# Queries and keys of a hybrid decoder layer by seven quadrant products (Strassen) on one Trainium2 core

## The chip, the core and the metric

The kernel runs on one core of a Trainium2 chip. The core has a matrix engine (TensorE, PE in the profile, with its weight loads as PEld), a vector engine (VectorE, DVE), an engine for copies and functions (ScalarE, ACT), GpSimd (POOL), and SyncE (SP), which here only issues transfers. The engines run side by side, each takes its own instructions in order, and they wait for one another by semaphores. PE reads from SBUF (on-chip memory of 128 partitions) and writes to PSUM, which has eight banks of 128 x 512 float32. GpSimd doesn't reach PSUM.

The metric is the device time of one execution in microseconds (us). A change of the time is given as after over before, below 1 for faster.

## The reference

One layer with 2048 tokens of width 1024, in float32. The projection is the part that the change touches; the rest of the layer follows it and is longer.

```python
hn = _rmsnorm(h, ln_mix[i])                  # h * rsqrt(mean(h*h) + eps) * gain
z = hn @ w_in[i]                             # (2048, 1024) @ (1024, 2048)
q = z[..., :512].reshape(B, S, 8, 64) * (64 ** -0.5)
k = z[..., 512:1024].reshape(B, S, 8, 64)
v = z[..., 1024:1536].reshape(B, S, 8, 64)
u = z[..., 1536:]
att = _dilated_attention(q, k, v, slopes)    # three window and dilation patterns
pool = _multiscale_pool(u, pool_w[i], pool_scale[i])
h = h + jnp.concatenate([att, pool], axis=-1) @ w_out[i]
...
```

`_multiscale_pool` takes, for four groups of 128 channels, the trailing mean over 2, 4, 8 or 16 tokens minus the token, multiplies it by a 128 x 128 matrix of the group and scales it per channel. After this come a gated MLP with a causal convolution and a gated addition of a per-layer embedding.

## The kernel before

All products are of float32 accuracy, made from three matmuls of a rounded type (float32r): each operand is kept as a high half (a rounded copy, made by ScalarE) and a low half (the operand minus its high half, made by DVE or GpSimd; `split`, L83). `mm3` (L88) adds high by high, high by low and low by high in one PSUM bank, so each product of 128 x 128 by 128 x 512 costs three matmuls, at L89, L90 and L91.

`phase_project` (L170) makes z. x lies transposed, channels on the partitions: eight k tiles of 128 channels by the tokens of a chunk. There are five chunks: two of 256 tokens, so that the start is short, then three of 512. For each chunk four groups of columns of w_in follow one another: 0 for queries, 1 for keys, 2 for values, 3 for the pooled channels (the last chunk takes 3 ahead of 2). A group is a loop over eight k tiles with four PSUM banks open (L303 to L316); in the groups 0, 1 and 3 w_in is the stationary operand and the tokens run past it, in group 2 it is the other way round, so that values come out with tokens on the partitions. A full group has 96 matmuls of 512 columns; in a chunk of 256 tokens the groups 0, 1 and 3 have 96 of 256 columns and group 2 has 48 of 512.

The high and low halves of the weights of groups 0 to 2 are made in the first chunk and stay in SBUF, in the pool a_w (L176), the phase's first; those of group 3 are fetched and split anew for each chunk. `ahead` (L271) keeps the splits three steps ahead of the matmuls and the fetches further. The order of PE, ACT, DVE and POOL in this phase is the order of the program text (L1947); transfers are issued by SP, those of the pooled branch by POOL.

The norm: `square` (L231) adds the squares of the next chunk, one k tile per step of group 1; `scale` (L235) sums them over the partitions with matmuls into the bank st, takes the root on GpSimd and prepares diagonal tiles; `spread_` (L239) spreads the root over the partitions by two matmuls (bc); `norm_a` (L242) multiplies x by it and `norm_b` (L246) makes the halves hnh and hnl, with the norm weight as the scale, one k tile per step of group 3. The first chunk is multiplied without its root, which is applied to the results (L349). A `Ticker` (L59) runs pieces of work some steps after they were entered; `pool_branch` (L410) puts its windowed sums, its halves, its product with pool_w (bank py, L456) and its stores on later steps with it.

After the phase its pools are closed, and attention's pool b_sb (L494) takes the same space in SBUF. Pools are laid one after another, tiles of a pool in the order in which their tags are first asked for, and a new tile waits until all that used its bytes before is done (reuse_waits). `load_qk` (L502) loads queries and keys of a head: qhh, ks, qll, and two tables of distances, fb and nb; the loads of head 0 come first (L748), those of values next.

Of the kernel before, what the change touches and what calls it, by code (L numbers as in the profile page):

```python
# [10 lines left out]
F32 = mybir.dt.float32  # L11
# [6 lines left out]
P = 128  # L18
# [147 lines left out]
ACFG = dict(nk=3, sc=5, ml=[[1,3,5,11],[1,3,5,7]], pq=[], ph=[1,2,4,8], fi=1, mn=[1,2],ld=4, lu=2, la=3, a0=1, low=[[[1, 0], [1, 1], [1, 1], [0, 0]], [[0, 0]] * 4, [[0, 0]] * 4], man=("PE", "ACT", "DVE", "POOL"))  # L166
EN = dict(PE=mybir.EngineType.PE, ACT=mybir.EngineType.Activation, DVE=mybir.EngineType.DVE, POOL=mybir.EngineType.Pool)


def phase_project(tc, g, xT, w_in, pool_w, rcnt):  # L170
    nc = tc.nc
    tk = g.ticker
    NZ, NV = 6, 3
    chunks = [(0, 256), (256, 256)] + [(t, CH) for t in range(CH, S, CH)]
    with ExitStack() as ctx:
        wres = ctx.enter_context(tc.tile_pool(name="a_w", bufs=1, reuse_waits="tile"))  # L176
        sb = ctx.enter_context(tc.tile_pool(name="a_sb", bufs=1, reuse_waits="tile"))
        psum = ctx.enter_context(tc.tile_pool(name="a_ps", bufs=6, space=PSUM, reuse_waits="tile"))
        psum1 = ctx.enter_context(tc.tile_pool(name="a_ps1", bufs=1, space=PSUM, reuse_waits="tile"))

        def small(name):
            return sb.tile([P, CH], F32, tag="raw", bufs=3, name=name)

        def zt(name):
            return sb.tile([P, CH], F32R, tag="z", bufs=NZ, name=name)
# [7 lines left out]
        g.f32r_tile = lambda pool: pool.tile([P, CH], F32R, tag="z", bufs=NZ, name="dg")  # L193

        def fetch(c, grp, k):
            i = (grp * KD + k) % 3 if c == 0 and grp < 3 else 0
            tag, bufs = (("raw", 3), ("wuh", 3), ("wul", 3))[i]
            raw = sb.tile([P, 512], F32R if i else F32, tag=tag, bufs=bufs, name=f"wr{grp}_{k}")
            raw = fp(raw) if i else raw
            nc.sync.dma_start(raw, w_in[k * P : (k + 1) * P, grp * 512 : (grp + 1) * 512])  # L200
            return raw

        def load_w(pool, raw, grp, k, tag, bufs, low=None):
            hi = pool.tile([P, 512], F32R, tag=tag + "h", bufs=bufs, name=f"wh{grp}_{k}")
            lo = pool.tile([P, 512], F32R, tag=tag + "l", bufs=bufs, name=f"wl{grp}_{k}")
            split(nc, hi, lo, raw, low)
            return hi, lo
# [5 lines left out]
        held = {}  # L213

        def loads(c):
            t0, n = chunks[c]
            st = Shared()
            st.n, st.xs, st.hn = n, [], []
            st.acc = sb.tile([P, CH], F32, tag="acc", name="acc")
            for hf in range(2):  # L220
                xt = sb.tile([P, 4, CH], F32, tag="x", bufs=2, name=f"x{c}_{hf}")
                m = 2 if c == 0 else 4
                for a in range(0, 4, m):
                    ka = slice(4 * hf + a, 4 * hf + a + m)
                    nc.sync.dma_start(xt[:, a : a + m, :n], xT[ka, :, t0 : t0 + n].rearrange("k p t -> p k t"))
                    if c == 0:
                        fetch_to(2 * hf + a // 2)
                st.xs += [xt[:, k, :] for k in range(4)]
            return st

        def square(st, k):  # L231
            eng = nc.gpsimd if st is first and k % 2 else None
            add_square(nc, sb, st.acc, st.xs[k][:, : st.n], k == 0, 1, zt if st is first else None, eng)

        def scale(st):  # L235
            st.pw = rms_scale(nc, g, psum1.tile([P, CH], F32, tag="st", name="st"), st.acc, st.n)
# [1791 lines left out]
```

## Time and profile before

| | |
|---|---|
| time, median of 3 runs | 2394.97 us (2390.77 to 2396.05) |
| the profiled execution | 2395.75 us, of which the span of the trace is 2394.0 |
| mean granted clock of PE | 0.987 |
| the projection phase in the trace | from 6.27 us (first matmul) to 400.07 (first matmul of attention) |
| matmuls with output z | 480 at each of L89 to L91 with tokens moving, 128 each with w_in moving |

The profile is of one execution. "Busy" is the time in which an engine has an instruction in work; PE's matmuls overlap, so that one of 512 columns is listed with some 390 ns though the next starts sooner. A row of a group gives line, engine and operation, output<-inputs by the names of the program, shapes and count, then busy time and mean duration, then idle time just ahead of it and what ended it. A row of the order in time gives start, duration, engine, line and operation, and in brackets the idle time before.

### The profile page before, as it was taken

Reading aid. Unit: us, or ns where it says so; the run is one execution under the profiler, and the core shown is the slowest. Engines: PE = TensorE matmul, PEld = TensorE weight load, DVE = VectorE, ACT = ScalarE, POOL = GpSimd, SP = SyncE. Lnnn points to the kernel's source line nnn. Section 1 sums busy time; section 2 is a strip of 40 time slices with the busy share of each in tenths; the row PEclk is TensorE's granted clock in tenths of the full one; section 3 lists DMA queues with packets and bytes.
Section 4 is the critical chain, followed back from the end, with each engine's and each line's share of the span. In section 5 each row is a group of like instructions: output and inputs, shape, how many; then the busy total and the mean of one; then the engine's idle time right before and its main releaser. Section 6 shows DMA issues by size and latency. Waiting matters only on the chain.

```text
span 2394.0 us, 32736 instructions
## 1 busy us (share of the span) xinstructions
PE 2320.2 (97%) x11251; PEld 1962.7 (82%) x11251; DVE 1714.3 (72%) x2684; ACT 1123.5 (47%) x2040; POOL 571.1 (24%) x552
## 2 busy tenths in 40 slices
PE   8999999999989989999999999999999999999998
PEld 7888887988868868888887787888878888888888
DVE  6645445888864668999999998777766565755665
ACT  5332234988832245454447353544444444444332
POOL 3322122356620133344430664000020000001000
PEclk9999999999999999999999999999999999999999
DMA  7534436877576664556567787444487776754332
GB/s 232 185 132 164 179 130 248 269 239 241 161 262 216 214 203 144 189 189 207 189 212 246 265 277 248 156 147 146 141 317 254 240 243 204 224 172 154 119 102 93
DMA packets 240550, 475.99 MB, mean 199 GB/s; under 512 B 37472, under 2 KB 63904, under 8 KB 237312
## 3 DMA queue, kind: packets, MB, share of 16 engines
q1 hardware_dynamic: 205040, 394.64, 50.2%
q0 software_dynamic: 15696, 51.49, 6.0%
q10 hardware_dynamic: 19648, 27.77, 3.3%
q8 instruction: 88, 1.44, 0.3%
q14 instruction: 78, 0.64, 0.1%
HBM read 309.14 MB, written 156.79 MB: 195 GB/s over the span
## 4 chain that ended last, share of the span: by engine, by line
PE 78%; DVE 8%; DMA 5%; issue 3%; ACT 1%; POOL 0%; SPq 0%; ACTq 0%; DVEq 0%; POOLq 0%
PE ua L1375 16%; PE uc L1375 8%; PE dn L89 5%; PE dn L90 5%; PE dn L91 5%; PE ub L1375 4%; PE z L91 4%; PE z L89 4%; PE z L90 4%; PE o L91 2%; PE o L89 2%; PE o L90 2%; PE tp L604 2%; PE gp L89 2%; PE gp L91 2%
## 5 line engine op out<-in xcount | busy, mean ns | idle before, releaser
L90 PE MATMUL dn<-al,wu 128*128 128x512 f32 x616 | 240.3, 390 | 3.2 <-DVE al L85 3.2
L89 PE MATMUL dn<-ah,wu 128*128 128x512 f32 x616 | 240.1, 390 | 0.0
L91 PE MATMUL dn<-ah,wu 128*128 128x512 f32 x616 | 239.8, 389 | 0.0
L85 DVE TENSOR_TENSOR al<-ra,ah 128x512 fp32r<-128x512 f32 x154 | 105.9, 690 | 110.0 <-ACT ah L84 107.8
L89 PE MATMUL z<-hnh,wh 128*128 128x512 f32 (+1 forms) x480 | 170.5, 355 | 10.8 <-ACT hnh L252 6.3
L90 PE MATMUL z<-hnl,wh 128*128 128x512 f32 (+1 forms) x480 | 170.3, 355 | 2.3 <-DVE hnl L253 2.0
L91 PE MATMUL z<-hnh,wl 128*128 128x512 f32 (+1 forms) x480 | 170.1, 354 | 2.3 <-POOL wl L85 1.7
L84 ACT CAST ah<-ra 128x512 fp32r<-128x512 f32 x154 | 95.2, 620 | 143.8 <-PE dn L91 124.9
L90 PEld LDWEIGHTS dn<-al,wu 128*128 128x128 f32 x616 | 115.6, 188 | 29.1 <-DVE al L85 5.2
L85 DVE TENSOR_TENSOR wu<-ru,wu 128x1024 fp32r<-128x1024 f32 x88 | 134.7, 1530 | 3.9 <-ACT wu L84 3.9
L89 PEld LDWEIGHTS dn<-ah,wu 128*128 128x128 f32 x616 | 115.6, 188 | 24.3 <-ACT ah L84 0.4
L91 PEld LDWEIGHTS dn<-ah,wu 128*128 128x128 f32 x616 | 115.6, 188 | 24.1
L1375 PE MATMUL ua<-s1h,wu 128*128 128x512 f32 x352 | 116.8, 393 | 4.4 <-ACT ug L1602 4.4
L1375 PE MATMUL ua<-s4h,wu 128*128 128x512 f32 x352 | 117.2, 394 | 2.6 <-ACT uv L1623 2.6
L1375 PE MATMUL uc<-a22h,wu 128*128 128x512 f32 x352 | 116.9, 393 | 2.7 <-DVE uv L1398 2.7
L1375 PE MATMUL ub<-a12h,wu 128*128 128x512 f32 x352 | 115.7, 389 | 1.1 <-ACT a12h L1431 1.1
L1375 PE MATMUL ua<-s2h,wu 128*128 128x512 f32 x352 | 115.8, 390 | 0.8 <-ACT ug L1576 0.7
L1375 PE MATMUL uc<-s3h,wu 128*128 128x512 f32 x352 | 115.7, 389 | 0.0
L1375 PE MATMUL ua<-a11h,wu 128*128 128x512 f32 x352 | 115.5, 389 | 0.0
L155 DVE TENSOR_TENSOR acc<-acc,sq 128x512 f32<-128x512 f32 (+1 forms) x125 | 81.3, 650 | 47.3 <-ACT sq L154 33.8
L85 DVE TENSOR_TENSOR wu<-rw,wu 128x512 fp32r<-128x512 f32 x149 | 101.1, 688 | 18.7 <-ACT wu L84 18.4
L89 PEld LDWEIGHTS z<-hnh,wh 128*128 128x128 f32 x480 | 94.5, 197 | 22.7 <-ACT hnh L252 6.3
(335 smaller groups left out, 6664.8 us busy)
## 6 DMA issues: line engine op xcount, KB each, us to landing
ru<-in_w_up_dram SPq DMA_DIRECT2D x66, 512.0 KB, 4.2
wr<-in_w_in_dram SPq DMA_DIRECT2D x64, 256.0 KB, 4.4
rw<-in_w_down_dram SPq DMA_DIRECT2D x61, 256.0 KB, 3.7
nt<-h SPq DMA_DIRECT2D x56, 256.0 KB, 3.9
td<-t SPq DMA_DIRECT2D x22, 512.0 KB, 2.6
t<-td SPq DMA_DIRECT2D x22, 512.0 KB, 3.7
nt<-in_w_down_dram POOLq DMA_DIRECT2D x44, 256.0 KB, 5.4
ra<-oq0s SPq DMA_DIRECT2D x44, 256.0 KB, 4.1
```

What stands on the lines that cost most here:

```text
L84: nc.scalar.copy(hi, src)
L85: (low or nc.gpsimd).tensor_tensor(lo, src, fp(hi), op=ALU.subtract)
L89: nc.tensor.matmul(ps, wh, ah, start=first, stop=False, skip_group_check=again)
L90: nc.tensor.matmul(ps, wh, al, start=False, stop=False, skip_group_check=again)
L91: nc.tensor.matmul(ps, wl, ah, start=False, stop=last, skip_group_check=again)
L155: nc.vector.tensor_tensor(acc[:, :n], acc[:, :n], sq[:, :n], op=ALU.add)
L604: nc.tensor.transpose(st.tp[:, bs], st.ee[:, bs], g.ident)
L1375: nc.tensor.matmul(pst, x[:, ksl], y, start=first and k == 0 and n == 0, stop=k == HK - 1 and n == 2, skip_group_check=True)
```

## The change

Queries and keys are no longer made chunk by chunk. The tokens are taken as four rows of 512, and two passes of `strassen` take two rows each: the 1024 x 1024 normalised tokens and the 1024 x 1024 first columns of w_in are each cut into four quadrants, and seven products of quadrants take the place of eight. One side of each product is a quadrant of the tokens (a) or a sum of such (s1 to s4), the other a quadrant of w_in (b) or a sum (t1 to t4). A product is four steps of 12 matmuls of 512 columns; a pass has 28 steps. A group of four banks (A, "chain") collects through four of the products, another (B: two free banks and the banks st and py) takes the other three; `kept` copies an intermediate out to SBUF, `whole` adds a bank to it and emits halves of q or k.

The norm weight is multiplied into w_in when it is split (`scaled_split`), and no longer into the tokens. The sums t are made once, in the steps of the groups (1, values), (1, pool) and (2, pool): 16 loads of w_in, 16 scalings on ScalarE, 16 subtractions on GpSimd, each stored to DRAM from GpSimd's queue, and they are fetched again in each pass. The sums s replace x in place: s1 on GpSimd, the others on DVE.

The order of the groups is now: values and pool of chunk 0, values and pool of chunk 1, pool and values of chunk 2, pass 0, pool and values of chunk 3, pass 1, pool and values of chunk 4. Squares of a next chunk are taken two per step in four steps. There is one SBUF pool, a_sb, in place of a_w and a_sb, and pw_h and pw_l are the first tiles asked for in it.

The core of the diff:

```diff
+QUADS = (
+    ("a11", "b11", True, True, (0, 0)),
+    ("a12", "b21", False, True, (0, 0)),
+    ("s2", "t2", True, False, (1, 0)),
+    ("s3", "t3", False, True, (1, 1)),
+    ("s1", "t1", True, False, (1, 1)),
+    ("a22", "t4", False, False, (1, 0)),
+    ("s4", "b22", True, False, (0, 1)),
+)
...
-        wres = ctx.enter_context(tc.tile_pool(name="a_w", bufs=1, reuse_waits="tile"))
         sb = ctx.enter_context(tc.tile_pool(name="a_sb", bufs=1, reuse_waits="tile"))
...
+        def scaled_split(hi, lo, raw, k, by_pool):
+            gain = g.vec[:, V_MIX + k : V_MIX + k + 1]
+            if by_pool:
+                nc.scalar.activation(raw, raw, AF.Copy, scale=gain)
+                split(nc, hi, lo, raw)
+            else:
+                nc.scalar.activation(hi, raw, AF.Copy, scale=gain)
+                nc.vector.scalar_tensor_tensor(lo, raw, gain, fp(hi), op0=ALU.mult, op1=ALU.subtract)
+
+        def prepare(key):
...
+            if gk is None:
+                split(nc, hi, lo, raw)
+            else:
+                scaled_split(hi, lo, raw, gk, kind != "x" and (k % 2 == 1 or c > 1))
+            held[(2, k) if kind == 2 else key] = hi, lo
+            if kind == "x":
+                pa, q = QUADS[k // HK][0], k % HK
+                if pa == "a22":
+                    operands[key] = chunk_of[2 * c + 1].hn[q + HK]
+                    return
+                ah, al = (tile_of("a" + x, 5, "a" + x, F32R) for x in "hl")
+                split(nc, ah, al, quad(c, pa, q), nc.vector)
+                operands[key] = ah, al
...
+            def subtract(n):
+                b11, b12, b21, b22 = b
+                o, x, y = ((b11, b12, b11), (b12, b22, b12), (b22, b22, b11), (b21, b21, b22))[n]
+                nc.gpsimd.tensor_tensor(o, x, y, op=ALU.subtract)
+                nc.gpsimd.dma_start(g.qd[q][("t1", "t3", "t2", "t4")[n]], o)
...
+        def strassen(p, nxt):
+            A = [ring("za") for _ in range(4)]
+            spare = [(nbank[0] + i) % 6 for i in (1, 2)]
...
+            def kept(j, x, src):
+                rs[x, j] = r = tile_of("r", 8, "r")
+                nc.scalar.copy(r, src)
+
+            def whole(j, x, src, emit, row):
+                r = rs.pop((x, j))
+                nc.vector.tensor_tensor(r, r, src, op=ALU.add)
+                emit(2 * p + row, j, r)
+
+            for m in range(28):
+                x, q = divmod(m, HK)
+                pa, wb, chain, starts, (row, col) = QUADS[x]
+                advance()
+                if x == 1 and q == 0:
+                    tk.flush()
+                if not chain and starts and q == 0:
+                    B = [special(t, "zb") for t in (f"p{spare[0]}", f"p{spare[1]}", "st", "py")]
+                bank = A if chain else B
...
+                for j in range(4):
+                    js = slice(j * P, (j + 1) * P)
+                    mm3(nc, bank[j], wh[:, js], wl[:, js], ah, al, starts and q == 0, q == HK - 1, not starts)
+                tk.tick()
+                if m < HK:
+                    nc.gpsimd.tensor_tensor(quad(p, "s1", m), quad(p, "a21", m), quad(p, "a22", m), op=ALU.add)
+                    nc.vector.tensor_tensor(quad(p, "s3", m), quad(p, "a11", m), quad(p, "a21", m), op=ALU.subtract)
+                if 0 < m <= HK:
+                    nc.vector.tensor_tensor(quad(p, "s2", m - 1), quad(p, "s1", m - 1), quad(p, "a11", m - 1), op=ALU.subtract)
+                if 6 <= m < 6 + HK:
+                    nc.vector.tensor_tensor(quad(p, "s4", m - 6), quad(p, "a12", m - 6), quad(p, "s2", m - 6), op=ALU.subtract)
+                if nxt:
+                    nxt(m)
...
+                            tk.later(1 + j, f)
...
+        def squares(st, k):
+            if k < 4:
+                square(st, 2 * k)
+                square(st, 2 * k + 1)
...
+        group(1, 2, hook)
...
+            squares(third, k)
+            norm_a(first, k)
+            if k == 4:
+                scale(third)
+            if k == 6:
+                spread_(third)
+            sums.pop(0)()
+
+        group(1, 3, hook)
...
+        def between(m):
...
+            if 4 <= m < 12:
+                norm_a(fourth, m - 4)
+            if 8 <= m < 12:
+                norm_b(fourth, m - 8)()
+            if 24 <= m:
+                norm_b(fourth, m - 20)()
...
+        strassen(0, between)
...
+        group(3, 3, hook)
...
+        group(3, 2, hook)
...
+        strassen(1, None)
+        group(4, 3, lambda k: None)
+        group(4, 2, lambda k: None)
```

More of the change, by code (lines that the diff above doesn't have):

```diff
@@ L191, in zpair @@
             return a[:, :n], zt(name + "l")[:, :n]
[L193 to L207, printed above, removed]
+        g.f32r_tile = lambda pool: zt("dg")
         pw_h = sb.tile([P, 4, P], F32R, tag="pwh", name="pw_h")
@@ L212, in phase_project @@
         tails = [sb.tile([P, 15], F32, tag=f"tail{q}", name=f"tail{q}") for q in range(4)]
-        held = {}
-        def loads(c):
-            t0, n = chunks[c]
[L217 to L221, printed above, removed]
+        order = []
+        for c in range(len(chunks)):
+            if c == 4:
+                order += [("x", 1, m) for m in range(28)]
+            for grp in (2, 3) if c < 2 else (3, 2):
+                order += [(grp, c, k) for k in range(KD)]
+            if c == 2:
+                order += [("x", 0, m) for m in range(28)]
@@ L286, in phase_project @@
+        def squares(st, k):
+            if k < 4:
+                square(st, 2 * k)
+                square(st, 2 * k + 1)
+        inv0 = []
+        first = loads(0)
+        first.row, first.off = 0, 0
         for k in range(ACFG["nk"]):
@@ new lines, in phase_project, with hook @@
+            norm(first, k, False)
+        def hook(k):
+            nonlocal second
+            squares(first, k)
+            if k == 2:
+                second = loads(1)
+                second.row, second.off = 0, 256
+            if k == ACFG["sc"]:
+                scale(first)
+            if k == KD - 1:
+                spread_(first)
+                rows[2] = [sb.tile([P, 4, CH], F32, tag="x", bufs=6, name="x2_0")]
+                inv0.append(rows[2][0][:, 0, :256])
+                nc.scalar.copy(inv0[0], first.inv)
+                first.inv = inv0[0]
@@ new lines, in phase_project, with hook @@
+        group(0, 3, hook)
+        for k in range(ACFG["nk"]):
+            norm(second, k)
+        third = None
+        def hook(k):
+            nonlocal third
+            if k == 1:
+                third = loads(2)
+                third.row, third.off = 1, 0
+            sums.pop(0)()
+        group(1, 2, hook)
+        def hook(k):
+            squares(third, k)
+            norm_a(first, k)
+            if k == 4:
+                scale(third)
+            if k == 6:
+                spread_(third)
+            sums.pop(0)()
@@ new lines, in phase_project, with hook @@
+        group(1, 3, hook)
+        for k in range(ACFG["nk"]):
+            norm(third, k)
+        fourth = None
+        def hook(k):
+            nonlocal fourth
+            if k == 1:
+                fourth = loads(3)
+                fourth.row, fourth.off = 2, 0
+            if sums:
+                sums.pop(0)()
+        group(2, 3, hook)
+        def hook(k):
+            squares(fourth, k)
+            if sums:
+                sums.pop(0)()
+        group(2, 2, hook)
+        assert not sums
@@ L414, in pool_branch @@
     cs = slice(t0, t0 + n)
-    u = sb.tile([P, HALO + CH], F32, tag="u", bufs=3, name="u")
+    u = sb.tile([P, HALO + CH], F32, tag="u", bufs=4, name="u")
     if c == 0:
```

386 lines of the change are left out of this document (232 added, 154 removed).

## The prediction, made before the change ran

> **What bounds the kernel now.** I read the page first, then the busy time by stretches, then the matmul groups and their order in time in the first 400 us, because the change lies there alone (the projection phase; attention begins at 400.07 us). Windows give busy us of each engine, the granted clock of PE, the DMA share and GB/s.
>
> ```profile
> span 2394.0 us, 32736 instructions
> ...
> PE 2320.2 (97%) x11251; PEld 1962.7 (82%) x11251; DVE 1714.3 (72%) x2684; ACT 1123.5 (47%) x2040; POOL 571.1 (24%) x552
> ```
>
> ```profile
> 6.27:29.30 23.03, 18.97 (x104) 17.87 (x105) 15.73 (x26) 10.36 (x23) 10.45 (x10) 0.85 0.66 232
> 29.30:125.60 96.30, 88.44 (x608) 82.54 (x607) 65.43 (x127) 45.26 (x95) 29.86 (x35) 0.96 0.62 198
> 125.60:399.30 273.70, 273.11 (x1217) 225.74 (x1215) 123.93 (x179) 81.23 (x143) 62.06 (x88) 1.00 0.43 160
> sum 393.03, PE 380.52 PEld 326.15 DVE 205.10 ACT 136.85 POOL 102.37; mean PE 126.84 PEld 108.72 DVE 68.37 ACT 45.62 POOL 34.12
> ```
>
> PE bounds the phase, but not evenly. From 125.60 to 399.30 us (the last three chunks) it is busy 273.11 of 273.70 us: no other engine matters there. Before 125.60 (the two half chunks of 256 tokens) it is not: up to 29.30 us it waits for its first operands and runs at a clock of 0.85, and from 29.30 to 125.60 it is busy 88.44 of 96.30 us. The busy column overstates PE, since matmuls overlap; what one costs is the distance from start to start. The groups say how many there are (each of the three lines of the split product has as many as L89):
>
> ```profile
> L89 PE MATMUL z<-hnh,wh 128*128 128x512 f32 x288 | 112.1, 389 | 0.0
> L89 PE MATMUL z<-hnh,wh 128*128 128x256 f32 x192 | 58.5, 304 | 10.8 <-ACT hnh L252 6.3 <-ACT wh L84 3.3 <-DVE qh L369 1.2
> L89 PE MATMUL z<-wh,hnh 128*128 128x512 f32 x128 | 50.3, 393 | 0.0
> ```
>
> ```profile
> 39.77 0.28 PE L91 MATMUL z<-hnh,wl 128*128 128x256 f32 x1
> ...
> 42.29 0.28 PE L91 MATMUL z<-hnh,wl 128*128 128x256 f32 x1
> ```
>
> ```profile
> 239.63 0.39 PE L89 MATMUL z<-hnh,wh 128*128 128x512 f32 x1
> ...
> 241.90 0.39 PE L90 MATMUL z<-hnl,wh 128*128 128x512 f32 x1
> ```
>
> From 39.77 to 42.29 us lie 21 starts of 256 columns, 0.120 us each; from 239.63 to 241.90 us ten of 512, 0.227 us each. A group of one chunk has 96 matmuls of q, k or pool (4 blocks, 8 k tiles, 3 lines), and 96 of values; a half chunk has 96 of 256 columns and, for values, 48 of 512. So the ideal time of 29.30 to 125.60 us (five groups of 96 x 0.120, two of 48 x 0.227, 12 small pool matmuls, and the two norms, about 2.2) is 57.6 + 21.8 + 1.4 + 2.2 = 83.0 us: 13.3 us are lost there, and almost nothing in the last three chunks.
>
> **PE's part of the change.** Removed: q and k of two half chunks, 4 x 96 x 0.120 = 46.1 us, and of three chunks, 6 x 96 x 0.227 = 130.8 us. Added: two times 28 steps of 12 matmuls, 672 x 0.227 = 152.5 us. That the stationary operand changes at every matmul is so before, too, so the distance stays. **Term: -24.4 us.** Values and pool keep their matmuls. This is the most that the change can win on PE, 1% of the time.
>
> **What the change puts beside PE.** The durations that I use (name, shape, count, busy, mean ns of one):
>
> ```profile
> L155 DVE TENSOR_TENSOR acc<-acc,sq 128x512 f32<-128x512 f32 x7 | 4.9, 693 | 4.4 <-ACT sq L154 4.4
> L155 DVE TENSOR_TENSOR acc<-acc,sq 128x256 f32<-128x256 f32 x7 | 2.9, 418 | 0.0
> L244 DVE TENSOR_TENSOR x<-x,bc 128x256 f32<-128x256 f32 x8 | 3.2, 408 | 0.0
> L430 DVE TENSOR_TENSOR ws<-u 128x270 f32<-128x270 f32 x4 | 1.7, 432 | 0.0
> ```
>
> ```profile
> L84 ACT CAST wh<-wr 128x512 fp32r<-128x512 f32 x29 | 17.1, 614 | 16.5 <-DMA wr<-in_w_in_dram 12.8 <-PE z L90 3.1 <-issue 0.6
> L154 ACT ACTIVATE sq<-x 128x512 f32<-128x512 f32 x7 | 4.4, 629 | 3.4 <-DVE acc L155 3.4
> L154 ACT ACTIVATE sq<-x 128x256 f32<-128x256 f32 x7 | 2.9, 417 | 0.7 <-DVE acc L155 0.7
> L374 ACT CAST kh<-z 128x256 fp32r<-128x256 f32 x8 | 2.6, 376 | 1.6 <-DVE z L352 1.6
> ```
>
> A step of DVE costs 0.69 us at 512 columns and 0.42 at 256; ScalarE 0.61 to 0.63 and 0.38 to 0.42. How a GpSimd subtraction stands beside DVE is decisive, because the change puts 16 subtractions of w_in quadrants, the low halves of 2 x 16 t tiles and 2 x 4 sums s1 on GpSimd. Here are DVE's steps of one norm beside three low halves of GpSimd:
>
> ```profile
> 24.87 0.17 DVE L118 CAST ph<-pw 128x2 fp32r<-128x2 f32 x1 [1.25 <-POOL pw L110]
> ```
>
> ```profile
> 100.48 1.26 DVE L118 CAST ph<-pw 128x4 fp32r<-128x4 f32 x1 [2.17 <-POOL pw L110]
> 101.78 1.20 DVE L119 TENSOR_TENSOR pl<-pw,ph 128x4 f32<-128x4 f32 x1
> 102.91 1.83 DVE L123 TENSOR_TENSOR dg<-ident,ph 128x512 fp32r<-128x512 f32 x1
> 104.66 0.68 DVE L123 TENSOR_TENSOR dg<-ident,pl 128x512 fp32r<-128x512 f32 x1
> ```
>
> ```profile
> 100.43 3.75 POOL L85 TENSOR_TENSOR wl<-wr,wh 128x512 fp32r<-128x512 f32 x3
> ```
>
> The same cast that takes 0.17 us alone takes 1.26, and the next one 1.20. The three GpSimd steps cost 3.75 us, DVE's four cost 0.17 + 0.17 + 0.68 + 0.68 = 1.70 alone (each as its like), and both are through in 105.34 - 100.43 = 4.91 us: 0.90 of the sum. So they nearly take turns. DVE steps with one input in PSUM don't:
>
> ```profile
> 209.79 0.68 DVE L244 TENSOR_TENSOR x<-x,bc 128x512 f32<-128x512 f32 x1
> ```
>
> ```profile
> 208.02 3.00 POOL L85 TENSOR_TENSOR wl<-wr,wh 128x512 fp32r<-128x512 f32 x2 [4.46 <-ACT wh L84]
> ```
>
> This one takes 0.68 us in the middle of GpSimd's run. I therefore charge 0.89 of the sum of GpSimd's steps (1.25 each) and of DVE's steps with two SBUF inputs. The Trainium skill (SBUF — State Buffer, section "SBUF: two separate sides") has the loser of that shared port pair blocked for the whole instruction. By that the sum would count in full and the two Strassen passes would lose some 10 us more, 2418 in all; the trace, at 0.90, bears out most of it but leaves the overheads overlapped.
>
> **Stage by stage** (V values, P pool, number of the chunk; X the two Strassen passes). The new order gives each half chunk only two groups, 22 us of PE instead of 46, but norms, squares and pooled sums of a half chunk stay as many.
>
> V0: its 8 weights and x tiles arrive as those of the first q group did, 6 matmuls of 0.227 use up a k tile as fast as 12 of 0.120, and GpSimd again makes half the low halves. Four extra in-place scalings (0.6 each) fit into ScalarE, busy 10.36 of 23.03 us. I take 0 (from -2 to 3). The 13.3 us lost from 29.30 to 125.60 us belong to the old order and go: **-13.3**, and new ones come:
>
> P0: the next chunk's squares come two to a step in four steps, and the fifth step's norm matmuls wait for them. ScalarE has eight squares (3.3), six weight copies (3.7), two value copies and pool_w's (1.8) ahead of it, DVE the last sum (0.4): 9.2 us against five steps of 12 x 0.120 = 7.2; with the spread two steps later, loss 3.5 (2 to 4). The stores of the values now stand in SP's queue ahead of the last three fetches of this stage; those are used 10 us later.
>
> V1: DVE's stream holds eight norms of (0.41, then 0.38 on ScalarE, then 0.42, with handovers 1.4) = 11.2 us, between them about 8 pooled steps of 0.43 and a wait for four scalings of w_in on ScalarE: some 16 us before the last k tile is ready, where PE needs 7 x 1.36 = 9.5. Loss 6.5 (3 to 7).
>
> P1: full-size squares now, two to a step, with one buffer between ScalarE and DVE. Their rhythm before:
>
> ```profile
> 90.06 0.63 ACT L154 ACTIVATE sq<-x 128x512 f32<-128x512 f32 x1 [0.76 <-DVE acc L155]
> ...
> 91.45 0.63 ACT L154 ACTIVATE sq<-x 128x512 f32<-128x512 f32 x1 [0.76 <-DVE acc L155]
> ```
>
> One takes 1.39 us, eight 11.1, and PE comes for them after 7.2 us. Ahead of them on DVE stand what is left of P0's pooled sums (about 13 x 0.43) and two value steps; beside them the scaling of the first half chunk (0.42 a step) and GpSimd's three subtractions and two low halves. With the least of this the loss is 6, with all of it taking turns 15; I take 10.5, the middle. While PE is late, GpSimd's 16 subtractions and DMA issues run on; nothing waits for them until the first t tile in X0.
>
> P2: eight norms of 512 columns, 0.68 + 0.61 + 0.69 + handovers = 2.1 us each in DVE's order, pooled steps of P1 between, GpSimd with a low half and a subtraction per step; PE takes 12 x 0.227 = 2.72 us per step. Loss 4 (1 to 8). V2, P3, V3, P4, V4: the work per step is that of the last three chunks before: 0.
>
> X0: 28 steps of 2.72 us. Step 12 reuses four PSUM banks whose sums DVE reads at steps 8 to 11, behind all it was given earlier: low halves of operands and weights, s3, s2, s4, the next chunk's scaling and half its norms, the pooled rest. By count that is 51 steps of 0.69 = 35.3 us up to the last bank, GpSimd 4 sums and 7 low halves, with the norm's power some 14.8: 0.89 x 50.1 = 44.6, against 12 x 2.72 + 2 = 34.7. Loss 10 (2 to 16). Afterwards DVE's list is shorter than PE's steps, and nothing is regained. X1 has no next chunk: 40 steps of DVE, 27.7, and nothing to some 5 us left of V3, GpSimd 13.8: 36.9 to 41.4, loss 4 (0 to 9). ScalarE has 88 copies of 0.61 in X0, 71% of it.
>
> DMA: 28 weights of 256 KB per pass are 92 GB/s over 76 us, and 16 loads and 16 stores in the early part add some 8 MB to windows that run at 198 GB/s; fetches reach six steps ahead. I take 0.
>
> Sum of the new losses: 3.5 + 6.5 + 10.5 + 4 + 10 + 4 = **+38.5 us**. The phase would then end where it ends now. The stores of q and k, before in every chunk, now leave during X0 and X1; the last ones lie two groups (44 us) ahead of the phase's end, as before.
>
> **What moves behind it.** The phase's pools disappear with it, and attention's pool takes their space from its start, in the order in which tiles are first asked for. Before, that start was the first weights of q, dead since the last q group; attention's q and k loads went out long before the phase ended:
>
> ```profile
> 360.53 0.58 SPq L56 DMA_DIRECT2D qhh<-qh  x1
> ...
> 363.61 0.45 SPq L56 DMA_DIRECT2D nb<-in_near_b_dram  x1
> ```
>
> ```profile
> qll<-ql SPq DMA_DIRECT2D x1, 1024.0 KB, 10.3
> nb<-in_near_b_dram SPq DMA_DIRECT2D x1, 128.0 KB, 9.5
> ```
>
> ```profile
> 399.84 0.40 PE L91 MATMUL py<-dh,pw_l 128*128 128x512 f32 x1
> 400.07 0.28 PE L573 MATMUL sn<-ks,qhh 128*128 128x256 f32 x1
> ```
>
> Now the first pool is the one that begins with pw_h and pw_l. The first load, qhh (8 KB a partition), covers both, and they are read by the very last matmuls of the phase (py, 399.84 us). So qhh waits for them, and ks, qll, fb and nb stand behind it in SP's queue. From the issue of qhh to the landing of qll took 361.80 + 10.3 - 360.53 = 11.6 us (qll issued two places behind), to that of nb 363.61 + 9.5 - 360.53 = 12.6. Before, the first score matmul followed py directly, at 400.07. **Term: +11.5 us** (7, if they land faster on empty queues, to 13). All engines are idle then. The v loads behind them are needed six steps later and stay hidden.
>
> The Trainium skill (TensorE: Matmul & The Clock Gate, section "What's actually happening") has PE at half clock after an idle window of about 3.4 us until it was busy for one. By that each of the two long waits (P1, attention's start) would cost about 1.7 us more, an estimate from that page, and the sum would be 2411; the stretch up to 29.30 us with its 0.85 agrees that waits cost clock.
>
> **Sum**, on the profiled execution of 2395.75 us (span 2394.0 and 1.75 around it, 0.8 over the median of 2394.97): 2395.75 - 24.4 - 13.3 + 38.5 + 11.5 = 2408.
>
> **Rivals.**
> 1. The vector work hides, and it is faster. If DVE and GpSimd overlap more than in the one row that I have, and queues run ahead while PE waits, the losses are near their lower ends, 2 + 3 + 6 + 1 + 2 + 0 = 14, and the loads cost 8.5: 2395.75 - 37.7 + 14 + 8.5 = 2380.5. It decides at step 12 of X0: a wait under 2 us there. For it speaks that DVE is busy only 205 us of the phase's 393 now; against it the row in which a cast waits out a GpSimd step.
> 2. The two halves cancel. Losses of two thirds of my sum, 26 us, end the phase 12 us earlier, and attention's loads take it back: 2395.75 - 37.7 + 26 + 11.5 = 2395.5, no change.
> 3. Everything takes turns: upper ends, 4 + 7 + 15 + 8 + 16 + 9 = 59, and 12 for the loads: 2429.
>
> **Chances.** The forecast (2400 to 2426) 0.52, the first rival (2375 to 2390) 0.27, the second 0.16, the third 0.05. A difference of 0.2%, 4.8 us, is about what a measurement can tell from none; so faster 0.28, same 0.17, slower 0.55. The range leaves out the third rival and the best of the first: 2381 to 2426. Cases of both signs hold much of the chance; the likeliest one's own range is 2400 to 2426.
>
> **What would show it.** Matmuls of z down by 288 from 1,824 in all three lines together; the distance of 0.227 us in X0 and X1; PE waiting in P0 and P1 for the norm (st, bc), in V1 for a low half of hn from DVE, at step 12 of X0 for a DVE read of a bank; DVE steps of 0.69 stretched to 1.2 beside GpSimd; qhh issued only after the last py, and 7 to 13 us without matmuls before the first score. Wrong, if X0 runs 28 steps in 76 us, or if qhh is issued before the phase ends.

## The result, and the profile after

The kernel after takes 2491.06 us (median of four executions, 2487.32 to 2491.85), the kernel before beside it 2393.1 (2390.77 to 2396.05). The ratio is 1.0406, 95% interval 1.0388 to 1.0424: 4% slower, at the far side of every case that the prediction wrote down. The profiled execution took 2490.68 us (span 2488.9); its first score matmul comes at 495.56 us in place of 400.07, 95.5 us later, and that is the whole difference.

The busy time of the kernel after, in windows that are the stages V0, P0, V1, P1, P2, V2, X0, P3, V3, X1 and then P4 with V4; behind the engines stand the granted clock, the DMA share and GB/s:

```profile
7.60:27.60 20.00, 16.34 (x54) 12.55 (x55) 15.47 (x25) 13.02 (x27) 10.42 (x10) 0.91 0.76 259
27.60:49.80 22.20, 15.62 (x104) 15.21 (x102) 9.85 (x20) 11.95 (x26) 6.74 (x13) 0.85 0.87 323
49.80:75.60 25.80, 17.97 (x57) 13.48 (x58) 18.50 (x41) 8.91 (x19) 8.35 (x11) 0.78 0.29 100
75.60:110.50 34.90, 19.61 (x111) 18.62 (x109) 25.40 (x32) 23.31 (x42) 22.39 (x23) 0.72 0.68 226
110.50:143.10 32.60, 25.77 (x106) 20.19 (x107) 25.17 (x34) 14.87 (x26) 20.71 (x29) 0.95 0.45 153
143.10:175.50 32.40, 27.18 (x110) 20.87 (x109) 21.38 (x33) 13.09 (x24) 10.07 (x20) 0.95 0.25 90
175.50:277.80 102.30, 88.44 (x351) 69.72 (x349) 72.18 (x91) 50.99 (x89) 32.15 (x26) 0.88 0.54 185
277.80:308.10 30.30, 25.46 (x105) 20.45 (x104) 15.44 (x24) 18.40 (x33) 11.22 (x12) 0.89 0.60 191
308.10:332.50 24.40, 24.40 (x109) 20.11 (x109) 18.86 (x30) 8.09 (x15) 3.28 (x9) 1.00 0.18 64
332.50:432.80 100.30, 84.87 (x341) 68.02 (x340) 66.35 (x81) 49.91 (x86) 32.28 (x26) 0.90 0.50 169
432.80:484.40 51.60, 47.54 (x205) 37.77 (x203) 22.15 (x32) 19.46 (x33) 15.39 (x23) 1.00 0.47 176
sum 476.80, PE 393.20 PEld 317.00 DVE 310.76 ACT 232.01 POOL 173.00; mean PE 35.75 PEld 28.82 DVE 28.25 ACT 21.09 POOL 15.73
```

And the whole phase of the kernel before in one window:

```profile
6.30:400.00 393.70, 381.19 (x1926) 326.73 (x1927) 205.60 (x332) 136.99 (x260) 102.86 (x134) 0.98 0.49 173
```

PE has fewer matmuls (10963 on the page, 288 fewer than before), yet the phase is 83 us longer. DVE's busy time rose from 205.60 to 310.76 us, GpSimd's from 102.86 to 173.00. Only V3 and the last 50 us run at full clock.

What PE waited for, from 0 to 520 us (total, times, longest):

```profile
PE st L100 <- DVE acc L155: 17.7, 3, 9.7
PE py L89 <- DVE mh L717: 13.0, 6, 3.5
PE za L89 <- DVE vt L506: 11.7, 2, 7.5
PE sn L828 <- DMA ks<-kk: 11.1, 1, 11.1
PE z L89 <- ACT hnh L354: 10.3, 3, 7.6
PE zb L89 <- DVE r L419: 10.1, 3, 4.5
PE z L89 <- DVE kl L403: 8.3, 3, 4.8
PE zb L90 <- DVE al L85: 6.1, 4, 4.9
```

Six of eight rows name DVE, on six different tiles. No single wait carries the loss; the same engine comes late in many places. Yet DVE isn't busy throughout: it works 310.76 of 476.80 us. What it waited for itself is mostly something that ScalarE makes ahead of it, a high half, a copy or a square (from 7.6 to 484.4 us, the four largest rows):

```profile
DVE kl L403 <- ACT kh L402: 23.3, 14, 4.8
DVE acc L155 <- ACT sq L154: 17.0, 19, 1.7
DVE vt L506 <- ACT vt L505: 16.4, 6, 5.7
DVE hnl L355 <- ACT hnh L354: 15.5, 20, 2.9
```

So the amount of work alone doesn't make DVE late: its list, taken in order, has pauses in it, too. PE's wait of 2.33 us on py at 63.82, for example, follows a pause of 2.90 in which DVE stood for hnh.

Two places show how DVE comes to be late. First P1, where PE comes for the norm's sums; PE, then DVE, then GpSimd in order of time:

```profile
88.51 0.28 PE L91 MATMUL z<-hnh,wl 128*128 128x256 f32 x1
98.52 1.65 PE L100 MATMUL st<-ones,acc 128*128 128x1 f32 x7 [9.72 <-DVE acc L155]
```

```profile
89.87 3.17 DVE L349 TENSOR_TENSOR x<-x,x 128x256 f32<-128x256 f32 x1
92.97 0.68 DVE L155 TENSOR_TENSOR acc<-acc,sq 128x512 f32<-128x512 f32 x1
94.34 1.13 DVE L155 TENSOR_TENSOR acc<-acc,sq 128x512 f32<-128x512 f32 x1 [0.69 <-ACT sq L154]
95.40 0.41 DVE L349 TENSOR_TENSOR x<-x,x 128x256 f32<-128x256 f32 x1
```

```profile
90.27 1.27 POOL L85 TENSOR_TENSOR wl<-wr,wh 128x512 fp32r<-128x512 f32 x1
91.48 1.27 POOL L383 TENSOR_TENSOR b<-b 128x512 f32<-128x512 f32 x1
```

The scaling that takes 0.41 us alone takes 3.17 beside two GpSimd operations (3.10 from its start to the next one's): 0.41 + 1.27 + 1.27 = 2.95 is the full sum, not 0.89 of it. The length agrees with the exclusive lock that the Trainium skill describes (SBUF — State Buffer, section "SBUF: two separate sides"). The Trainium skill gives the pair to the operation that starts first, though; here DVE's recorded start, 89.87, lies ahead of GpSimd's, 90.27, and DVE still was the one held up.

Second, step 12 of X0, where the prediction had put its decision; DVE, then PE:

```profile
221.55 0.67 DVE L419 TENSOR_TENSOR r<-r,zb 128x512 f32<-128x512 f32 x1
222.93 0.69 DVE L394 SCALAR_TENSOR_TENSOR ql<-r,qh 128x512 fp32r<-128x512 f32 x1 [0.70 <-ACT qh L393]
223.53 0.68 DVE L443 TENSOR_TENSOR x<-x,x 128x512 f32<-128x512 f32 x1
224.13 1.75 DVE L349 TENSOR_TENSOR x<-x,inv 128x512 f32<-128x512 f32 x1
225.81 0.68 DVE L355 TENSOR_TENSOR hnl<-x,hnh 128x512 fp32r<-128x512 f32 x1
226.41 0.68 DVE L85 TENSOR_TENSOR al<-x,ah 128x512 fp32r<-128x512 f32 x1
227.02 0.67 DVE L419 TENSOR_TENSOR r<-r,zb 128x512 f32<-128x512 f32 x1
```

```profile
227.75 0.79 PE L89 MATMUL zb<-ah,wh 128*128 128x512 f32 x1 [4.50 <-DVE r L419]
232.61 0.80 PE L89 MATMUL zb<-ah,wh 128*128 128x512 f32 x1 [3.22 <-DVE r L419]
```

From one addition that frees a bank to the next DVE needs 227.02 - 221.55 = 5.47 us, where a step of PE has 2.72. One of the operations in between takes 1.75 us in place of 0.68, and one waits 0.70 for ScalarE.

Then the clock. PE at the start of X0, and two windows behind the wait:

```profile
176.63 0.39 PE L91 MATMUL za<-ah,wl 128*128 128x512 f32 x1
181.27 0.80 PE L89 MATMUL za<-ah,wh 128*128 128x512 f32 x1 [4.25 <-DVE vt L506]
181.86 0.63 PE L90 MATMUL za<-al,wh 128*128 128x512 f32 x1
182.29 0.63 PE L91 MATMUL za<-ah,wl 128*128 128x512 f32 x1
```

```profile
181.30:190.40 9.10, 9.10 (x26) 7.46 (x27) 4.36 (x9) 3.58 (x7) 3.35 (x4) 0.50 0.97 390
190.40:195.00 4.60, 4.60 (x21) 3.78 (x20) 2.79 (x5) 1.48 (x3) 1.73 (x3) 1.00 1.03 339
```

Behind the wait of 4.25 us products start 0.43 us apart in place of 0.227, at a granted clock of 0.50 for 9.1 us: 17 products of 512 columns lie there, so the wait costs some 17 x 0.2 = 3.4 us a second time. The half clock after an idle stretch is what the Trainium skill says of it (TensorE: Matmul & The Clock Gate, section "What's actually happening"). The lengths differ: the Trainium skill has an idle window of about 3.4 us ahead of the half clock and about as much busy time end it. Here the half clock lasts 9.1 us, and behind the waits of only 2.46 us (at 163.20) and 2.33 us (at 388.78) products start 0.43 us apart, too, for some 3 us, while behind that of 2.84 (at 124.00) they don't.

### The profile page after: what moved, and what is told of

Same layout as the page of the kernel before. It is cut to its first block, busy times and chain, and to the rows that moved or that the text cites. A ratio compares the mean times of both kernels' runs of the same rounds, so it can differ in the third digit from the quotient of the medians.

```text
span 2488.9 us, 32623 instructions
## 1 busy us (share of the span) xinstructions
PE 2328.8 (94%) x10963; PEld 1949.7 (78%) x10963; DVE 1811.6 (73%) x2788; ACT 1219.1 (49%) x2197; POOL 643.8 (26%) x616
## 4 chain that ended last, share of the span: by engine, by line
PE 66%; DVE 7%; DMA 5%; issue 3%; ACT 2%; POOL 1%; SPq 0%; POOLq 0%; DVEq 0%; ACTq 0%
PE ua L1630 15%; PE uc L1630 8%; PE dn L90 5%; PE dn L89 5%; PE dn L91 5%; PE ub L1630 4%; PE o L91 2%; PE o L89 2%; PE o L90 2%; PE tp L859 2%; PE gp L89 2%; PE gp L91 2%; PE gp L90 2%; DVE wu L85 1%; PE o L901 1%
## 5 line engine op out<-in xcount | busy, mean ns | idle before, releaser
L85 POOL TENSOR_TENSOR wl<-wr,wh 128x512 fp32r<-128x512 f32 x68 | 92.1, 1355 | 162.0 <-ACT wh L84 140.2
L927 POOL TENSOR_TENSOR s<-s,ev 64x512 f32<-64x512 f32 x60 | 76.7, 1285 | 139.0 <-DMA s<-ev 114.1
L84 ACT CAST wu<-rw 128x512 fp32r<-128x512 f32 x149 | 90.8, 616 | 32.0 <-DMA rw<-in_w_down_dram 18.2
L89 PE MATMUL o<-mh,hwo 128*128 128x512 f32 x256 | 101.4, 396 | 5.3 <-ACT hwo L84 5.3
```

What stands on the lines that cost most here:

```text
L84: nc.scalar.copy(hi, src)
L85: (low or nc.gpsimd).tensor_tensor(lo, src, fp(hi), op=ALU.subtract)
L89: nc.tensor.matmul(ps, wh, ah, start=first, stop=False, skip_group_check=again)
L927: sums.later(3, lambda: nc.gpsimd.tensor_tensor(dst[mine], dst[mine], t[mine], op=ALU.add))
```

## The experiments

Theories: **vector** (DVE, with GpSimd holding it up, has more to do than the stages last, so its lateness turns up wherever PE next needs it), against **places** (single hand-overs, buffers or points in PE's order that could be moved), **clock** (PE's slow clock is a cost of its own), and **loads** (for the stretch ahead of attention). "Before" is 2393 us in each comparison. Runs 2 to 7 and 10 are one execution each, so a few us of theirs mean nothing; the others are medians of four.

**1. The pooled weights' place.** The four lines move:

```diff
-        pw_h = sb.tile([P, 4, P], F32R, tag="pwh", name="pw_h")
...
         first = loads(0)
+        pw_h = sb.tile([P, 4, P], F32R, tag="pwh", name="pw_h")
...
```

> The changed kernel with the four small tile declarations (pw_h, pw_l, rc, tails) moved behind the first loads of x, so that attention's first load takes the bytes of x, dead since the second pass, and not those of pw_h. Theory (the load of qhh waits for the last py matmul): qhh is issued during the last two groups, the first score matmul follows py at once, the 11.1 + 3.5 us of waits at 484 us go, and the whole is 13 to 16 us faster than the changed kernel, about 2476. Rival (attention's start is bound by its value loads or by its vector work anyway): the waits go there, and it is less than 5 us faster. The projection phase itself stays as it is.

2477.33 us (2472.87 to 2479.51, ratio to before 1.0353, 1.033 to 1.0376): 13.7 less than after. The phase ends as it did, and the wait of 11.1 on ks is gone. The loads' theory holds.

**2. A fourth buffer for the values.**

```diff
-    NZ, NV = 6, 3
+    NZ, NV = 6, 4
...
-            tag, bufs = (("raw", 4), ("ah", 5), ("al", 5))[i % 3 if i < 2 * KD else 0]
+            tag, bufs = (("raw", 4), ("ah", 4), ("al", 4))[i % 3 if i < 2 * KD else 0]
```

> Four buffers for value tiles in place of three (ah and al four in place of five, for the space). Theory A (the fourth value tile of a group waits until the first one's store has landed, ScalarE and DVE stand still, and PE finds its banks unread at the start of a pass): PE's two waits for vt at the starts of the passes, 4.25 and 7.45 us, go, and with them some us of slow clock: 10 to 16 us faster than the changed kernel. Rival B (DVE is behind by its list, the store only happens to be the last thing): the wait comes back at the next read of a bank or operand, under 4 us faster.

2484.05 us, 7 less, between the two; but the waits on vt stayed (11.7, the longest 7.4). What they wait for is DVE's backlog, not the first tile's store: ahead of X0 of the kernel after, DVE works from 171.80 to 182.41 us with one pause of 1.31, and the values' low halves stand last in that list. The places theory falls here; where the 7 us come from isn't shown.

**3. GpSimd's t work left out.**

```diff
-                nc.gpsimd.tensor_tensor(o, x, y, op=ALU.subtract)
                 nc.gpsimd.dma_start(g.qd[q][("t1", "t3", "t2", "t4")[n]], o)
...
             if gk is None:
-                split(nc, hi, lo, raw)
+                nc.scalar.copy(hi, raw)
```

> Leaves out the 16 subtractions of quadrants of w_in on GpSimd (unsubtracted tiles are stored) and the low halves of the 32 t tiles (the third matmul of mm3 takes the high half again); matmuls, transfers and DVE's own list stay. Theory L (DVE and GpSimd shut each other out, and this stretches DVE's list): DVE's steps in the passes are 0.69 instead of up to 1.8, PE's waits and slow clock in chunk 1's two groups, chunk 2's two and both passes fall by half or more, the phase ends 30 us or more earlier, the whole about 2455. Rival O (DVE's list, its waits for ScalarE and the fixed places of bank reads in PE's order are enough): less than 15 us.

2456.3 us, 34.8 less. The page gives GpSimd 576.4 us busy (643.8 in after), and DVE 1774.3 (1811.6) for the same 2788 instructions: 67 us of GpSimd's work had stretched DVE's by 37. The first row is the operands' low half in after, the second the same in this run (times 7.6 to 484):

```profile
L85 DVE TENSOR_TENSOR al<-x,ah 128x512 fp32r<-128x512 f32 x48 | 41.4, 866 | 11.2 <-ACT ah L84 11.2
```

```profile
L85 DVE TENSOR_TENSOR al<-x,ah 128x512 fp32r<-128x512 f32 x48 | 32.8, 685 | 15.7 <-ACT ah L84 15.7
```

X0 falls from 102.3 to 90.8 us, and the stages ahead of it end 15 us earlier.

**4. The next row's norms later in X0.**

```diff
-            if 4 <= m < 12:
-                norm_a(fourth, m - 4)
-            if 8 <= m < 12:
-                norm_b(fourth, m - 8)()
+            if 12 <= m < 20:
+                norm_a(fourth, m - 12)
+            if 16 <= m < 20:
+                norm_b(fourth, m - 16)()
```

> Moves the next chunk's scaling in pass 0 from steps 4 to 11 to steps 12 to 19, and the first four of its halves from steps 8 to 11 to steps 16 to 19. Theory (DVE's list between steps 4 and 12 holds too much ahead of the four bank reads): PE's waits for r at steps 12 (4.5 and 3.2 us) fall under 2 in all, pass 0 takes 90 to 95 us instead of 102, the whole is 7 to 12 us faster. Rival (DVE is short in the whole pass): the same work makes PE wait later, under 4 us.

2481.53 us, 9.5 less; X0 takes 93.8 us, and the waits on r fall from 10.1 to 5.5, those at step 12 from 7.7 to 3.2, not under 2.

**5. PE kept busy where it waits.** Products that nobody reads:

```diff
+        def fill(n):
+            f = special("st", "fill")
+            for _ in range(n):
+                nc.tensor.matmul(f, g.onesr, held[2, 0][0], start=True, stop=True)
+
         def scale(st):
+            fill({256: 20, 512: 36}[st.n] if st is second or st is third else 0) if st is not first else None
...
+            fill((15, 28)[p])
             for m in range(28):
```

> 99 extra products of 512 columns (g.onesr by the first value weight, into the bank "st", read by nobody) stand where TensorE waits longest: 20 ahead of the norm sums of the second half of row 0 (wait 5.35 in the trace of after), 36 ahead of those of row 1 (9.72), 15 and 28 ahead of the two Strassen passes (4.25 and 7.45). At 0.227 us of one at full clock they take 22.5 us, about what the four waits take (26.8), so by themselves they cost nothing. Theory clock (the waits pull the granted clock down, and the roughly 50 us of slow products in the phase come from that): TensorE stays busy, the products behind run faster, the phase ends 10 to 20 us earlier, 2471 to 2481. Rival VectorE: the clock rises, but what TensorE gains it waits for the next line of VectorE; the time stays within 4 us of 2491. Rival no link: the slow part (time of the products over 0.227 us each) stays, the time is 0 to 6 longer.

2491.55 us: no change. The window of P0 as above (the stage itself ends at 47.3 in this run) and that of X0:

```profile
27.60:49.80 22.20, 19.98 (x134) 17.82 (x133) 11.47 (x25) 12.73 (x28) 6.83 (x13) 1.00 0.88 327
177.30:275.10 97.80, 83.76 (x351) 65.56 (x350) 70.05 (x88) 48.65 (x86) 31.73 (x26) 0.95 0.57 194
```

The clock rises from 0.85 to 1.00 in P0 and from 0.88 to 0.95 in X0, so the waits do cause it; X0 ends 2.7 us earlier than in after. It is lost again at X1: its filler waited 15.1 us for DVE to read the bank st, the pass began 21 us later, and then took 84.1 us in place of 100.3. Given a head start, DVE keeps up. V3 and X1 together took 133.0 us, against 124.6. The time is the one of the rival "VectorE"; but the wait on st is one that the filler itself put there, so what a full clock alone would give at X1 isn't shown, and up to the end of X0 it gave 2.7 us.

**6. The pooled product later.** `fi` goes from 1 to 3.

> The pooled branch's small product is issued three steps behind its low half instead of one. Theory place (the product stands in TensorE's order where its operand or its bank is just late, 21.6 us of waits on py in after): these waits fall below 8 us and the time falls by 10 to 15, to 2476-2481. Rival throughput (VectorE has more to do than the stage lasts, wherever the product stands): the waits on py fall, but the ones on st, z and zb rise by about as much, and the time stays within 4 us of 2491.

2488.99 us, 2.1 less. The waits on py, which both theories had fall, did not fall; on mh and ml alone they are 18.9 + 8.5 = 27.4 (13.0 + 3.7 in after). The theory of the place falls, as far as the step of issue goes. These are waits until DVE has read the one bank py; a second bank for it was not tried.

**7. Without the quadrant sums.** The four `tensor_tensor` for s1 to s4 in `strassen` are taken out.

> Leaves out the four sums s1 to s4 of quadrants of the normed input: in each pass 4 additions on GpSimd and 12 subtractions on VectorE (about 0.6 us each, 7 us per pass). Theory list (VectorE's list at steps 0 to 12 of a pass is what TensorE waits for): X0 falls from 102.3 by 6 to 9, X1 from 100.3 by 2 to 4, the time by 8 to 13 to 2478-2483. Rival hand-over (banks and the values' copies at the start of the passes set the time, the sums lie in between): under 4 us together.

2475.65 us, 15.4 less, more than expected: X0 92.8 us, X1 88.7. I had put 2 to 4 on X1, and it gained 11.6. That the sums also delay what DVE brings along from V3 is a likely reason, not a shown one.

**8. Edits 1, 3 and 4 together.**

> Three edits together: pooled weights declared behind the first loads (13.7 us alone), no GpSimd subtractions and low halves of the t quadrants (left out; 34.8 alone), norms of the next row in the later steps of X0 (9.5 alone). If they are independent: 58 us in all, 2433. If the second and third take away the same waits (both relieve VectorE in X0): 2437 to 2443. In either case more than 30 us over the kernel before: the seven products lose to what VectorE has of its own. Rival (GpSimd's hold on VectorE is all of it, and the rest follows it): below 2410.

2444.41 us (2442.17 to 2448.86, ratio 1.0214, 1.0191 to 1.0238): 46.7 of the 58 us, just past the upper case. X0 is 88.5 us, 2.4 under edit 3 alone: edits 3 and 4 take away the same waits. Still 51 us over before.

**9. The order without Strassen.** Eight products of quadrants per pass, row by row, on the same banks (the helper for t and the sums go):

```diff
-QUADS = (
...
+PRODS = (
+    ("a21", "b11", 0, True),
+    ("a22", "b21", 0, False),
+    ("a21", "b12", 1, True),
+    ("a22", "b22", 1, False),
+    ("a11", "b11", 0, True),
+    ("a11", "b12", 1, True),
+    ("a12", "b21", 0, False),
+    ("a12", "b22", 1, False),
+)
...
-        strassen(0, between)
+        eight(0, between)
...
-        strassen(1, None)
+        eight(1, None)
```

> The new order alone: values and pooled branch first as in after, but queries and keys of each 1024 tokens by all eight products of quadrants (32 steps in place of 28). TensorE has the 24.4 us more that Strassen saves; gone are the four subtractions on GpSimd of each quadrant and their stores, the low halves of t on GpSimd, the sums s1 to s4, the additions of kept products, and 8 of 24 operand splits in a pass. Theory order (half the loss stands in the stages ahead of X0, which keep all norms, squares, values and pooled work but have lost the query and key products beside them): X0 begins at about 160, as in the run without GpSimd's t work (V0 to V2 there end 15 us earlier than in after), each pass takes 87 us of products and some 5 of waits, and with P3, V3, P4, V4 as in after the phase ends at about 448: 2450 to 2460, still 55 to 65 over before. Rival Strassen's additions: without them VectorE has room everywhere, the early stages close up too, and the time is that of before plus the later attention loads, 2393 + 15 or less.

2435.68 us (2431.78 to 2441.1, ratio 1.0175, 1.0151 to 1.0198). It also moves the next row's halves in the first pass from the steps 8 to 11 to the steps 16 to 19, and its load to step 23. The early stages, the two passes and the whole phase:

```profile
7.90:149.10 141.20, 111.47 (x536) 93.10 (x537) 97.29 (x181) 74.21 (x146) 49.23 (x72) 0.92 0.50 172
149.10:243.20 94.10, 91.03 (x398) 75.05 (x397) 56.29 (x88) 49.10 (x84) 7.53 (x8) 0.98 0.64 210
290.30:384.10 93.80, 89.64 (x389) 73.72 (x388) 48.49 (x73) 46.07 (x78) 6.05 (x7) 0.98 0.64 208
7.90:431.40 423.50, 385.93 (x1734) 318.81 (x1734) 250.10 (x412) 205.39 (x369) 88.35 (x126) 0.96 0.54 181
```

This run lies between both theories and divides the loss. Passes of 32 steps take 94 us, less than Strassen's 28 steps with 102 and 100. With PE's work of before, the new order alone costs 42 us (14 of them would be the loads); Strassen on top of it costs 55, although it saves PE 24. These 55 us include the earlier place of the halves in the first pass; run 4, which moves them and the scaling, gained 9.5.

**10. One window sum of each.**

```diff
-        while have < w:
+        while have < min(w, 2):
```

> Leaves out all but the first of the doubling sums of each pooled window (30 of 50 additions of line 685 on VectorE, 22.5 us busy in the trace of after); nothing else changes. Theory throughput (VectorE is the bound of the early stages): the stages P0 to V2 together fall by 8 to 14, P3 and P4 by some 3 more, the time by 11 to 18, to 2473-2480, and the waits on acc and py fall most. Rival place (TensorE waits for a chain of single operations, not for the amount): under 5.

2471.99 us, 19.1 less, for 22.5 us of DVE's work: some 0.85 of each microsecond comes out in the time. Throughput holds, with two misses: the gain is a little larger than expected, and it isn't the waits on acc (17.7 to 15.1) and py (21.6 to 19.8) that fall most, but those on vt (11.7 to 5.9) at the starts of the passes. X0 and X1 are 4.5 and 5.3 us shorter, which agrees with work carried over into them.

**11. The disputed vector work all out.** Edits 1, 3, 7 and 10, and:

```diff
-                split(nc, ah, al, quad(c, pa, q), nc.vector)
-                operands[key] = ah, al
+                nc.scalar.copy(ah, quad(c, pa, q))
+                operands[key] = ah, ah
```

> Seven products per pass as in after, the pooled weights declared behind the first loads, and the disputed vector work left out at once: GpSimd's subtractions and low halves of t, the sums s1 to s4, the low halves of the quadrant operands (the high half stands in for them), and all but the first sum of each pooled window. TensorE issues the same products. Theory vector work (TensorE's saving is there, and the phase is as long as VectorE and GpSimd need): the passes fall to 80 to 86 us each for 78 of products, P3 below 27, X0 begins at about 140, the phase ends near 400 to 408, the time is 2385 to 2405. Rival (bank hand-overs, the slow clock or the order of TensorE itself hold a large part): passes above 90, the time above 2415.

2403.46 us (2400.99 to 2409.53, ratio 1.0058, 1.0039 to 1.0078), inside the theory's range:

```profile
146.10:226.80 80.70, 79.02 (x351) 64.72 (x349) 36.56 (x56) 49.99 (x88) 5.47 (x7) 1.00 0.72 238
279.30:359.40 80.10, 77.46 (x340) 63.49 (x340) 29.43 (x43) 47.34 (x82) 4.29 (x6) 1.00 0.65 215
```

The passes run at full clock, 27 us shorter than the eight products of run 9; 2 x 4 x 2.72 = 22 of these are the steps saved, the rest fewer waits. So PE's saving is real, and it shows when this vector work is gone. X0 begins at 146.1 us, not at about 140, and P3 missed its mark (28.2 us, not under 27): it still waits for banks that DVE reads at the pass's end. The time stays above before, because the stages up to X0 still take 138 us.

**12. The order alone, repaired.** Run 9 with edit 1, four buffers in place of five in the operand rings, and three for the squares:

```diff
-            add_square(nc, sb, st.acc, st.xs[k], k == 0, 1, zt if st is first else None, eng)
+            add_square(nc, sb, st.acc, st.xs[k], k == 0, 3, zt if st is first else None, eng)
```

> The order alone with eight products (2435.7 measured) with the pooled weights declared behind the first loads (13.7 us in after) and three buffers in place of one for the squares, which ScalarE and VectorE hand to and fro one at a time ahead of the norm's sums (waits on acc 13.6 us there); the operand rings go from five to four to make room. Theory chain (the early stages of the new order wait for this hand-over, not for the amount of vector work): the waits on acc fall below 8, the time to 2414-2418. Rival amount: the waits on acc stay or turn up at the norms, 2420 to 2424. By either it stays over the kernel before by more than 0.8%.

2420.61 us (2415.56 to 2423.91, ratio 1.0115, 1.0093 to 1.0137). The waits on acc fall from 13.6 to 10.6 and X0 begins 5 us earlier, but the median is the rival's; two of the four runs lie below 2420, so this is a narrow verdict. What keeps the early stages at 137 us for 95 us of products is not settled: DVE is busy 99.57 us there and GpSimd 49.86, together more than the stages last; but DVE is idle for 37 us of them, and only one of its hand-overs with ScalarE, that of the squares, was loosened here.

## Why the prediction was right in sign and far off in size

The loss of a stage is its length less its products at 0.227 us (512 columns) or 0.12 (256), from the first start in it to the first of the next; "slow" is what remains when the waits are taken off.

| stage | predicted loss | measured | of it waits | slow |
|---|---|---|---|---|
| P0 | 3.5 | 10.1 | 6.6 | 3.5 |
| V1 | 6.5 | 13.8 | 7.8 | 6.0 |
| P1 | 10.5 | 21.9 | 15.3 | 6.6 |
| P2 | 4 | 9.7 | 6.8 | 2.9 |
| V2 | 0 | 8.2 | 5.1 | 3.1 |
| X0 | 10 | 24.3 | 13.9 | 10.5 |
| P3 | 0 | 8.0 | 4.8 | 3.2 |
| X1 | 4 | 23.4 | 15.4 | 8.0 |
| V3, P4, V4 | 0 | 5.4 | 3.9 | 1.5 |
| sum | 38.5 | 124.8 | 79.6 | 45.2 |

The terms that are left are small. Beside the 13.3 us that were to go, the phase before lost 12.7 (10.8 up to 29.30 us, 1.9 behind 125.60), where V0 now loses 8.6; the first product comes 1.4 later; attention waits 11.1 in place of 11.5. So the predicted sum becomes 2408 + 86.3 - 4.1 + 1.4 - 0.4 = 2491.2; the profiled execution took 2490.68. The table holds the whole error.

- **PE -24.4:** right. 288 matmuls fewer, and 27 us between the passes of runs 9 and 11, of which 22 are the steps saved.
- **Attention's loads +11.5:** right. In the trace qhh went out at 484.48 us, behind the last small product, PE waited 11.1, and run 1 took 13.7 away.
- **The squares at P1 and the bank at step 12 of X0:** the right places. Step 12 waited 4.50 + 3.22 = 7.7 us where 10 was predicted; P1 waited 9.72 for acc. For V1 the place was wrong: its 7.8 us of waits are all on the pooled product (py), none on a low half of hn.
- **"Afterwards DVE's list is shorter than PE's steps, and nothing is regained", and 0 for V2, P3 and P4:** this step failed. I compared DVE's list with PE's steps up to one named wait and let DVE begin each stage with an empty list, but for the "nothing to some 5 us left of V3". What was left at a stage's end was paid at the next hand-over: 4.25 and 7.45 us on vt at the start of X0 and X1, 4.84 on kl at the start of P3, and some 21 us on the pooled product, which the prediction did not name. Runs 2 and 6 moved two such places and the waits stayed; runs 3, 7 and 10 took work away, and with it went 34.8, 15.4 and 19.1 us, though most of the waits grew shorter rather than went (on vt from 11.7 to 10.1, 8.8 and 5.9).
- **"I therefore charge 0.89 of the sum":** too little in P1's row, which took the full sum and 0.15 us more (3.10 against 2.95). By the full lock of the Trainium skill the prediction would have been 2418, so the rate is only a small part of the error.
- **The clock, 3.4 us in a side sentence and 0 in the sum:** mis-sized. I counted two long waits; behind the first product of the phase there are 31 over half a microsecond, even short ones (2.33 and 2.46 us) among those with slow starts behind them, and 45 us of slow products. Run 5 shows that waits cause it; the 2.7 us that it had gained by the end of X0 were lost at X1, where its filler waited for DVE.
- **The third rival, "Everything takes turns", 2429:** the nearest to what happened, given 0.05. Its upper ends add up to 59 of 124.8; they too were taken stage by stage, and without the clock.
- **"The vector work hides":** excluded by X0's wait at step 12; run 11 shows that it would have needed most of the added work to vanish.

The sign came out right for the reason given and not by luck: without the losses of the stages the other terms come to 24.4 + 13.3 - 11.5 = 26.2 us faster, and the losses outweigh them. But the forecast had 38.5 of the 124.8 us, less than a third.

One sum would have been a warning. DVE and GpSimd are busy 310.76 + 173.00 = 483.8 us in the phase after; less the 37 us by which part of GpSimd's work stretches DVE (run 3), that is an estimated 447, where the phase before lasted 394 with 308.5. As far as the two take turns, such a list leaves no room for the forecast. It is no bound: a DVE step that read a bank took its 0.68 us in the middle of GpSimd's run (the prediction's row at 209.79), and in run 9 the sum is 250.10 + 88.35 = 338.5 in a phase of 423.5 that is late as well. There the stages tell more: 97.29 + 49.23 = 146.5 in early stages of 141.2, which keep their vector work and have lost the query and key products beside it. How much of DVE's lateness is its work and how much its pauses for ScalarE stays open.

## What to carry to other kernels

A saving of matmuls that is paid in vector work is to be judged by the work of VectorE and GpSimd beside it, over the whole phase and stage by stage, with what is left of one stage carried into the next, and not by the lists between single waits. If a wait stays or moves when its place is changed (runs 2, 5, 6) and the time falls when work is left out (runs 3, 7, 10), look to that engine's list, its pauses included, before another buffer. An edit that reorders a phase and changes its arithmetic is best run in halves: run 9 gave 42 us to the order and 55 to Strassen with its places, and neither could be read from the sum.

## What the runs showed of the hardware

- GpSimd's cost to VectorE: 67 us of GpSimd's element-wise work taken away made the same 2788 VectorE instructions 37 us shorter (run 3); a single scaling of 0.41 us took 3.17 beside two of GpSimd's.
- The slow clock needs no long pause: a wait of 4.25 us was followed by 9.1 us at 0.50, waits of 2.33 and 2.46 us were followed by some 3 us of starts 0.43 us apart, and P1, with 15.3 us of waits in 35, ran at a mean of 0.72. Idle products in the wait of P0 brought it from 0.85 to 1.00 (run 5), and the whole time stayed (2491.55 us against 2491.06).
